# Gate rows by way of DRAM, six inner values read back during "up", the last two chunks of "down" multiplied bank by bank

## Chip, cores and metric

The kernel runs on one core of a Trainium2 chip. The metric is the device time of one execution in microseconds (us); the time of a kernel is the median of its runs.

## What is computed

One transformer block of 512 tokens (S) and width 2048 (D), in fp32: adaptive layer norm from a condition vector c, a mixer of short convolution and sparse attention, and a gated feed-forward part of width 5632 (FF). The change touches where the two gate vectors g_a and g_f come in, and the last product.

```python
sh_a, sc_a, g_a, sh_f, sc_f, g_f = jnp.split(jax.nn.silu(c) @ ada_w[l] + ada_b[l], 6, axis=-1)
...
x = x + g_a[:, None, :] * (jnp.concatenate([y_conv, y_attn], axis=-1) @ w_out[l])
h = modulate(rms_norm(x, norm_ffn[l]), sh_f, sc_f)
x = x + g_f[:, None, :] * ((jax.nn.silu(h @ ffn_w1[l]) * (h @ ffn_w3[l])) @ ffn_w2[l])
```

## The kernel before

Every large fp32 product is done in three TensorE products of a split operand: ScalarE casts a high part (`whi` of a weight, `phi` of an activation), VectorE subtracts it for the low part (`wlo`, `plo`), and TensorE adds low·high, high·low and high·high into one PSUM bank.

The stages follow each other: the mixer with its projections, the output product with w_out ("o", about 705 to 893 us), the second norm, the gated pair w1, w3 ("up", 905 to 1782), and w2 ("down", to the end).

**"o" and "down"** share the function `products`. It splits both operands into 2 x 2 blocks and forms seven block products (passes p = 1, 5, 6, 3, 7, 2, 4) for each group of chunks of 128 rows: two groups of four chunks in "o", four groups of 6, 6, 5 and 5 in "down". The unit of the order is a step (group b, pass p, chunk k): 12 matmuls, three for each of four banks (`multiply`, L965). Two passes run in turn on two sets of four banks, called main and aux. For a step two places ahead the function emits the split of the activation (`a_split`: for p = 5 a difference `u` of the tiles g1 and g0, L935, and always `phi` L946 and `plo` L947) and of the weight (`w_split`: `whi` L919, `wlo` L921), and a GpSimd DMA (L927, queue POOL) that adds the next weight block to the weight tile in place. `start_loads` issues the weight and g loads on SyncE's queue (SP), each as soon as its ring has room. The rings hold three `whi` and `wlo` and six of the activation's parts. A scheduler then orders the instructions of each engine; an engine takes them strictly in that order.

**In "up"**, the units u = 0 to 43 run passes of the same kind on the normed activations `hC` (L1187 with whi, L1189 with wlo). Their results, 44 tiles `d` of 128 x 512, go to DRAM (`gd`), and "down" reads them back as g0 and g1 (L1419), seven of each at a time. These rings lie in memory that the operands of "up" use, the block `hC1` (pool stack `hst`) among them; `hC1` is last used by the last step with p = 1.

**The gates.** Each gate vector exists first as columns (`gac`, `gfc`: 128 partitions x 16). The product with a token-major result needs it as rows, the same 2048 values in all 128 partitions (`ga`, `gf`). `gate_rows` makes them: for each of 16 blocks VectorE forms a diagonal matrix `dg` (L291), TensorE multiplies a matrix of ones with it (L292; the profile counts two TensorE rows for each), and ScalarE copies each finished bank (L293). It is called in a hook at (b, p, k) = (0, 7, 2) of "o" with bank set main, and at (0, 1, 1) of "down" with aux. `ga` is first read when the first results of "o" are scaled, `gf` in the last group of "down". At the end, the last pass (p = 4) of the last group multiplies each bank by `gf` (L1435), adds it to y (L1436) and stores it (L1441).

Of the kernel before, what the change touches and what calls it, by code (L numbers as in the profile page):

```python
# [10 lines left out]
F32 = mybir.dt.float32  # L11
# [3 lines left out]
ALU = mybir.AluOpType  # L15
# [3 lines left out]
P = 128  # L19
D = 2048  # L20
S = 512
# [50 lines left out]
def block_kernel(ctx: ExitStack, tc: tile.TileContext, a: dict, out: bass.AP):  # L72
# [153 lines left out]
    def sums_stream():  # L226

        jobs = [(lambda acc, n=n: gate_cols(acc, n, 0, gac), 2 * D + n * 512) for n in range(4)]
        for j in range(8):
            m = 1 - j % 2  # L230
            jobs.append((lambda acc, m=m, j=j: ada_cols(main if j == 7 else aux, acc, 1, m, j // 2 * 4, 4), (3 + m) * D + j // 2 * 512))
        at_job, late = 0, None
        for e, (turn_, c0) in enumerate(jobs):
            acc = accp.tile([P, 512], F32, tag=f"acc{e % 2}", name=f"acc{e % 2}")
            for k in range(KC):
                w = spare[0]()
                with tc.issue_after(latest["load"]):
                    nc.sync.dma_start(w, ada_v[:, k, c0:c0 + 512])
                with tc.issue_after(latest["lo"]):
                    if k:  # L240
                        nc.vector.scalar_tensor_tensor(acc, w, cT[:, k:k + 1], acc, op0=ALU.mult, op1=ALU.add)
                    else:
                        nc.vector.tensor_scalar(acc, w, cT[:, k:k + 1], None, op0=ALU.mult)
                if late and k == 2:
                    late[0](late[1])
                yield
            late = turn_, acc
        late[0](late[1])

    def gate_steps(temp, lag):  # L250

        for n in range(4):
            acc = accp.tile([P, 512], F32, tag="acc0", name="acc0")
            for k in range(KC):
                w = temp() if k else acc
                with tc.issue_after(latest["load"]):
                    nc.sync.dma_start(w, ada_v[:, k, 5 * D + n * 512:5 * D + (n + 1) * 512])
                for _ in range(lag // 2):
                    yield
                with tc.issue_after(latest["hi"]):  # L260
                    nc.scalar.activation(w, w, AF.Copy, scale=cT[:, k:k + 1])
                if k:
                    nc.gpsimd.dma_start(acc, w, accum_op=ALU.add)
                for _ in range(lag - lag // 2):
                    yield
            gate_cols(acc, n, 1, gfc)

    def gate_cols(acc, n, which, to):

# [12 lines left out]
            nc.vector.tensor_reduce(d, v, axis=AX, op=ALU.add, negate=True)  # L282
            nc.vector.tensor_sub(d, d, b)

    def gate_rows(row, col, tile_of, temp):

        for n in range(4):
            ps = tile_of()
            for c in range(4):
                dg = temp.tile([P, P], F32, tag="dg", name="dg", bufs=2)  # L290
                nc.vector.tensor_scalar(dg, ident, col[:, 4 * n + c:4 * n + c + 1], None, op0=ALU.mult)  # L291
                nc.tensor.matmul(ps[:, c * P:(c + 1) * P], ones, dg, start=True, stop=True)  # L292
            nc.scalar.copy(row[:, n * 512:(n + 1) * 512], ps)  # L293

    pp = pool("ps", 4, space=PSUM)
    main = lambda: pp.tile([P, S], F32, tag="main", name="main")
# [573 lines left out]
    qk.close()  # L870
    act_.close()

    dram = ctx.enter_context(tc.tile_pool(name="spill", bufs=1, space=bass.MemoryType.DRAM))
    xd = [dram.tile([P, NT, 512], F32, name=f"xd{n}") for n in range(4)]
    gd = [dram.tile([P, S], F32, name=f"gd{f}") for f in range(FF // P)]
    HS, HK = S // 2, KC // 2
# [1 line left out]
    BLOCK = {1: (0, 0), 2: (0, 0), 5: (1, 1), 7: (1, 1), 6: (0, 1), 3: (0, 1), 4: (1, 0)}  # L878
    FIRST, LAST = (1, 5, 6, 4), (2, 7, 3, 4)

    def products(w, groups, order, flip, new_w, room, T, t_loads, G0, G1, g_loads, parts_, sums, read, hook):

        steps = [(b, p, k) for b, (top, _) in enumerate(groups) for p in order[b] for k in range(len(top))]
        where = {s: i for i, s in enumerate(steps)}
# [10 lines left out]
        for b, (top, _) in enumerate(groups):  # L895
            for p in (3, 2):
                for k in range(len(top)):
                    loads["w"].append(((b, 7 if p == 3 else 2, k), lambda n, b=b, p=p, k=k: load_w(n, b, p, k)))
        begun = {q: 0 for q in loads}

        def start_loads(done, most, which=("g0", "t", "g1", "w")):

# [47 lines left out]
        def multiply(i):  # L950

            b, p, k = steps[i]
            n_k = len(groups[b][0])
            chain = "x" if p in (1, 6, 7, 4) else "y"
            begins = p in (1, 5, 2) and k == 0
            ends_ = p in (4, 3, 2) and k == n_k - 1
            if begins:
                make = main if (chain == "x") == (b % 2 == flip) else aux
                banks[chain] = [make() for _ in range(4)]
            wt, at_k = split_w.pop(i), split_a.pop(i)  # L960
            for e, ps in enumerate(banks[chain]):
                tok = slice((e // 2) * P, (e // 2 + 1) * P)
                cs = slice((e % 2) * 512, (e % 2 + 1) * 512)
                for m, (l, r) in enumerate(((0, 1), (1, 0), (0, 0))):
                    nc.tensor.matmul(ps, at_k[l][:, tok], wt[r][:, cs], start=begins and m == 0, stop=ends_ and m == 2,  # L965
                                     skip_group_check=True)
            note("mm")
            if k == n_k - 1:
                reads.extend((b, p, e, ps) for e, ps in enumerate(banks[chain]))
# [133 lines left out]
    def o_hook(b, p, k):  # L1103

        if (b, p, k) == (0, 1, 0):
            with tc.issue_after(latest["o_hi"]), tc.issue_after(latest["o_lo"]):
                next(rest[0])
        if (b, p, k) == (0, 1, 1):
            with tc.issue_after(latest["o_lo"]):
                next(stream, None)  # L1110
        if (b, p, k) == (0, 7, 0):
            next(rest[0], None)
        if (b, p, k) == (0, 7, 2):
            gate_rows(ga, gac, main, tp)
        if b and p == 2:
            scaled()
        if b and p == 7:
            if k == 0:
                for i in (2, 3):
                    for n in range(2):  # L1120
                        cs = slice(n * 512, (n + 1) * 512)
                        nc.vector.tensor_mul(y2[:, i, cs], y2[:, i, cs], ga[:, cs])
                        nc.gpsimd.dma_start(y2[:, i, cs], x[i * P:(i + 1) * P, cs], accum_op=ALU.add)
            scaled()
            for _ in range((1, 2, 2, 3)[k]):
                x2_store(*turns.pop(0))
        if b and p == 4:
            if k == 0:
                row_norms(0)
            scaled()  # L1130
            x2_store(*turns.pop(0))
            if k > 1:
                modulated(0, 0, 4 * k - 8, aux)
                split_half(0, 0, 4 * k - 8)
# [235 lines left out]
    t2p = pool("t2", 1, stack=ust)  # L1370
    gtp = pool("gate", 1, stack=ust)
    gate = gate_steps(lambda: gtp.tile([P, 512], F32, tag="graw", name="graw"), 4)
    for n, s in enumerate(order):
        for m in range(n + 5, n + 1, -1):
            if m < len(order) and lead[id(order[m])] == m - n:
                prepare(m, "sum")
        if n + 5 < len(order):
            begin(order[n + 5]["u"])
        if n > 2:
            prepare(n + 2, "split")  # L1380
        if n < 4 * PLAIN:
            h_sums(n)
        s["mm"](s, (1,) if n < 3 else (0, 1)) if n < 4 * PLAIN else s["mm"](s)
        if 0 < n < 3:
            prepare(n + 2, "split")
        s["post"](s)
        if n >= 8 * PLAIN:
            next(gate, None)
    for _ in gate:
        pass  # L1390
    ust.close()
    hst.close()


    GROUPS, at0 = [], 0
    for n in (6, 6, 5, 5):
        GROUPS.append((range(at0, at0 + n), range(at0 + n, at0 + 2 * n)))
        at0 += 2 * n
    GM = 6
    pap = pool("parts", 6)  # L1400
    rgp = pool("graw", GM + 1)
    xsp = pool("xsum", GM + 1)
    wxp = pool("wraw", 5)
    yp = pool("y2", 1)
    y2 = yp.tile([P, NT, D], F32, name="y2")
    gf = yp.tile([P, D], F32, name="gf")
    tp = pool("tmp2", 4)
    T, G0, G1 = {}, {}, {}

    def load_t(b, k):  # L1410
        pair = big()
        for e in range(min(2, len(GROUPS[b][0]) - k)):
            T[b, k + e] = pair[:, e * 1024:(e + 1) * 1024]
            f = GROUPS[b][0][k + e]
            nc.sync.dma_start(T[b, k + e], w2[f * P:(f + 1) * P, 0:1024])

    def load_g(to, j, b, k):
        to[b, k] = rgp.tile([P, S], F32, tag=f"g{j}", name=f"g{j}")
        nc.sync.dma_start(to[b, k], gd[GROUPS[b][j][k]])  # L1419

    every_k = [(b, k) for b, (top, _) in enumerate(GROUPS) for k in range(len(top))]
    t_loads = [((b, 4, min(k + 1, len(top) - 1)), lambda n, b=b, k=k: load_t(b, k))
# [23 lines left out]

    def d_hook(b, p, k):

        if (b, p, k) == (0, 1, 1):
            gate_rows(gf, gfc, aux, tp)  # L1450
        if (b, p, k) == (len(GROUPS) - 1, 7, 0):
            for i in (2, 3):
                for n in range(2):
                    cs = slice(n * 512, (n + 1) * 512)
                    nc.vector.tensor_mul(y2[:, i, cs], y2[:, i, cs], gf[:, cs])
                    nc.gpsimd.dma_start(y2[:, i, cs], xd[n][:, i, :], accum_op=ALU.add)

    products(w2, GROUPS, ((1, 5, 6, 3, 7, 2, 4),) * 4, 0,
             lambda n: (ring[0] if n % 9 in (0, 2, 4, 6) else wxp).tile([P, 1024], F32, tag="raw", name="raw"),
             {"t": 4, "w": 9, "g0": GM + 1, "g1": GM + 1}, T, t_loads, G0, G1, g_loads, pap, xsp, d_read, d_hook)  # L1460


# [22 lines left out]
```

## Time and profile before

| what | us |
|---|---|
| median of three runs | 2224.24 |
| their spread | 2221.83 to 2224.64 |
| the profiled execution's own time | 2223.04 |
| its span | 2221.3 |

The span runs from the first to the last instruction of the profiled execution; about 1.7 us of its own time lie outside it. In the profile, PE is TensorE's matmul side and PEld its weight loads, DVE is VectorE, ACT ScalarE, POOL GpSimd, SP SyncE (SPq: the time it takes to issue). A row of a timeline has its start, its length, the engine, the line, the operation with output and inputs, the partitions and elements, a count, and in brackets how long the engine stood idle before and what ended that wait. A row of the chain of waits has a start, a length and what the end of the program hung on in that stretch. The figure in PEclk is the clock that TensorE was granted, as a share of full speed.

### The profile page before, as it was taken

Reading aid. Unit: us, or ns where it says so; the run is one execution under the profiler, and the core shown is the slowest. Engines: PE = TensorE matmul, PEld = TensorE weight load, DVE = VectorE, ACT = ScalarE, POOL = GpSimd, SP = SyncE. Lnnn points to the kernel's source line nnn. Section 1 sums busy time; section 2 is a strip of 40 time slices with the busy share of each in tenths; the row PEclk is TensorE's granted clock in tenths of the full one; section 3 lists DMA queues with packets and bytes.
Section 4 is the critical chain, followed back from the end, with each engine's and each line's share of the span. In section 5 each row is a group of like instructions: output and inputs, shape, how many; then the busy total and the mean of one; then the engine's idle time right before and its main releaser. Section 6 shows DMA issues by size and latency. Waiting matters only on the chain.

```text
span 2221.3 us, 30757 instructions
## 1 busy us (share of the span) xinstructions
PE 2150.8 (97%) x10999; PEld 1805.2 (81%) x10999; DVE 1797.8 (81%) x2795; ACT 1110.0 (50%) x1863; POOL 273.5 (12%) x321
## 2 busy tenths in 40 slices
PE   5899999999999999899999999999999989999998
PEld 5677778878778787788888888888888878888887
DVE  5888868878878787698888888888888876878787
ACT  6545334554543554745555555555554455554543
POOL 2330000000000223101110110110110021211132
PEclk9999999999999999999999999999999999999999
DMA  8885775645558968366665665666665399898897
GB/s 296 293 264 173 236 245 177 187 140 150 153 169 250 227 147 182 114 183 171 175 172 161 166 163 155 170 163 165 172 165 149 128 265 232 212 229 204 223 183 181
DMA packets 387550, 421.57 MB, mean 190 GB/s; under 512 B 19808, under 2 KB 293572, under 8 KB 386884
## 3 DMA queue, kind: packets, MB, share of 16 engines
q1 hardware_dynamic: 352068, 316.82, 45.8%
q0 software_dynamic: 35328, 102.78, 23.5%
q8 instruction: 86, 1.41, 0.3%
q14 instruction: 68, 0.56, 0.1%
HBM read 383.87 MB, written 19.92 MB: 182 GB/s over the span
## 4 chain that ended last, share of the span: by engine, by line
PE 82%; DVE 6%; DMA 6%; issue 3%; ACT 1%; POOL 1%; SPq 0%; DVEq 0%; POOLq 0%; ACTq 0%
PE main L1187 15%; PE aux L1187 11%; PE main L965 10%; PE aux L965 10%; PE main L1189 8%; PE aux L1189 6%; PE main L108 5%; PE main L110 5%; PE main L109 5%; PE aux L783 2%; DMA t<-in_w_out 1%; PE aux L755 1%; DMA y<-in_x 1%; DVE acc L326 1%; DMA raw<-in_w_in 1%
## 5 line engine op out<-in xcount | busy, mean ns | idle before, releaser
L1187 PE MATMUL main<-hC,whi 128*128 128x512 f32 x1408 | 355.1, 394 | 0.0
L1187 PEld LDWEIGHTS main<-hC,whi 128*128 128x128 f32 x1408 | 253.6, 189 | 46.0 <-DVE hC L1054 0.5
L1187 PE MATMUL aux<-hC,whi 128*128 128x512 f32 x1072 | 268.6, 392 | 0.0
L1187 PEld LDWEIGHTS aux<-hC,whi 128*128 128x128 f32 x1072 | 192.6, 189 | 34.0
L1180 DVE TENSOR_TENSOR wlo<-xy,whi 128x1024 fp32r<-128x1024 f32 x135 | 164.5, 1219 | 64.3 <-ACT whi L1174 64.2
L1174 ACT CAST whi<-xy 128x1024 fp32r<-128x1024 f32 x135 | 141.5, 1048 | 146.8 <-PE main L1187 76.8
L108 PE MATMUL main<-alo,whi 128*128 128x512 f32 x448 | 185.4, 414 | 22.0 <-DVE alo L396 22.0
L1189 PEld LDWEIGHTS main<-hC,wlo 128*128 128x128 f32 x1408 | 192.2, 190 | 14.3
L1189 PE MATMUL main<-hC,wlo 128*128 128x256 f32 x1408 | 196.2, 282 | 0.0
L109 PE MATMUL main<-ahi,wlo 128*128 128x512 f32 x448 | 179.2, 400 | 0.0
L110 PE MATMUL main<-ahi,whi 128*128 128x512 f32 x448 | 179.1, 400 | 0.0
L965 PE MATMUL main<-wlo,phi 128*128 128x512 f32 x420 | 167.1, 399 | 12.3 <-ACT phi L946 4.5
L965 PE MATMUL main<-whi,phi 128*128 128x512 f32 x420 | 166.0, 395 | 0.0
L965 PE MATMUL main<-whi,plo 128*128 128x512 f32 x420 | 166.0, 395 | 0.0
L965 PE MATMUL aux<-wlo,phi 128*128 128x512 f32 x420 | 164.3, 391 | 0.0
L965 PE MATMUL aux<-whi,plo 128*128 128x512 f32 x420 | 163.6, 390 | 0.0
L965 PE MATMUL aux<-whi,phi 128*128 128x512 f32 x420 | 163.5, 389 | 0.0
L1189 PEld LDWEIGHTS aux<-hC,wlo 128*128 128x128 f32 x1072 | 146.2, 190 | 10.5
L919 ACT CAST whi<-raw 128x1024 fp32r<-128x1024 f32 x90 | 94.9, 1055 | 114.7 <-PE aux L965 60.0
L1174 ACT CAST whi<-t 128x1024 fp32r<-128x1024 f32 x84 | 88.2, 1049 | 123.1 <-PE aux L1187 63.2
L919 ACT CAST whi<-xy 128x1024 fp32r<-128x1024 f32 x88 | 92.9, 1055 | 113.4 <-PE main L965 55.4
L1189 PE MATMUL aux<-hC,wlo 128*128 128x256 f32 x1072 | 149.5, 282 | 0.0
(341 smaller groups left out, 4488.7 us busy)
## 6 DMA issues: line engine op xcount, KB each, us to landing
xy<-in_ffn_w SPq DMA_DIRECT2D x130, 512.0 KB, 4.8
raw<-in_ffn_w SPq DMA_DIRECT2D x112, 512.0 KB, 5.1
araw<-in_ada_w SPq DMA_DIRECT2D x208, 256.0 KB, 4.0
xy<-in_ffn_w POOLq DMA_DIRECT2D x66, 512.0 KB, 6.3
raw<-in_w_in SPq DMA_DIRECT2D x128, 192.0 KB, 2.9
raw<-in_w_in SPq DMA_DIRECT2D x40, 512.0 KB, 6.0
xy<-in_ada_w SPq DMA_DIRECT2D x80, 256.0 KB, 4.3
graw<-in_ada_w SPq DMA_DIRECT2D x60, 256.0 KB, 2.8
```

What stands on the lines that cost most here:

```text
L108: nc.tensor.matmul(ps, lhs[0], rhs[1], start=first, stop=False)
L109: nc.tensor.matmul(ps, lhs[1], rhs[0], start=False, stop=False)
L110: nc.tensor.matmul(ps, lhs[0], rhs[0], start=False, stop=last)
L326: nc.vector.scalar_tensor_tensor(acc, w, s, acc, op0=ALU.mult, op1=ALU.add)
L755: nc.tensor.matmul(one[b], queries(g, i, h), kT[b][g][:, :L], start=True, stop=True)
L783: nc.tensor.matmul(po[:, b * HD:(b + 1) * HD], s["pT"][b][:, kb * P:(kb + 1) * P], vv[b][:, kb, g * HD:(g + 1) * HD], start=kb == 0, stop= ...
L919: nc.scalar.copy(hi, wt)
L965: nc.tensor.matmul(ps, at_k[l][:, tok], wt[r][:, cs], start=begins and m == 0, stop=ends_ and m == 2, skip_group_check=True)
L1174: nc.scalar.copy(hi, t)
L1180: nc.vector.tensor_sub(lo, t, hi.bitcast(F32))
L1187: nc.tensor.matmul(ps, wt[0][:, ks[k]], hC[p][:, k, :], start=first and k == 0, stop=False, skip_group_check=True)
L1189: nc.tensor.matmul(ps[:, HS:], wt[1][:, ks[k]], hC[p][:, k, 0:HS], start=False, stop=last and k == HK - 1, skip_group_check=True)
```

## The change

There are three parts.

1. `gate_rows` is gone. `gate_out` turns the columns by one TensorE transpose (128 x 16 to 16 x 128), VectorE copies the result into a free accumulator, and a GpSimd DMA stores its 8 KB in DRAM (`grow`). `gate_in` is one SyncE DMA that reads `grow` into all 128 partitions (1 MB written). For `ga`, `gate_out` stands in the stream that sums the gates during attention, `gate_in` at step (0, 6, 0) of "o". For `gf`, `gate_out` follows the last gate columns in "up", and `gate_in` stands at step (1, 1, 0) of "down".
2. `hst` is closed right after the last step with p = 1 in "up" instead of after "up". The g0 ring gets a pool of its own in that memory, and its first six loads are issued there; `products` is told by `begun` that six are under way. The g1 ring stays where both were.
3. In `multiply`, the last step but one returns at once, and the last step does both chunks bank by bank: six matmuls for the first bank, then six for the next.

```diff
+    def gate_out(which, col, psum_tile, acc):
+        ps = psum_tile()
+        nc.tensor.transpose(ps[:KC, :P], col, ident)
+        gt = acc[:KC, 0:P]
+        nc.vector.tensor_copy(gt, ps[:KC, :P])
+        nc.gpsimd.dma_start(grow[which].rearrange("o (k p) -> (o k) p", p=P), gt)
+
+    def gate_in(which, row):
+        nc.sync.dma_start(row, grow[which].to_broadcast([P, D]))
...
                 if late and k == 2:
                     late[0](late[1])
+                    if e == 4:
+                        gate_out(0, gac, aux, late[1])
...
             gate_cols(acc, n, 1, gfc)
+        gate_out(1, gfc, main, acc)
...
-        begun = {q: 0 for q in loads}
+        begun = {q: (begun or {}).get(q, 0) for q in loads}
...
-            wt, at_k = split_w.pop(i), split_a.pop(i)
+            if i == len(steps) - 2:
+                return
+            at_once = (i - 1, i) if i == len(steps) - 1 else (i,)
             for e, ps in enumerate(banks[chain]):
                 tok = slice((e // 2) * P, (e // 2 + 1) * P)
                 cs = slice((e % 2) * 512, (e % 2 + 1) * 512)
-                for m, (l, r) in enumerate(((0, 1), (1, 0), (0, 0))):
-                    nc.tensor.matmul(ps, at_k[l][:, tok], wt[r][:, cs], start=begins and m == 0, stop=ends_ and m == 2,
-                                     skip_group_check=True)
+                for j in at_once:
+                    wt, at_k = split_w[j], split_a[j]
+                    for m, (l, r) in enumerate(((0, 1), (1, 0), (0, 0))):
+                        nc.tensor.matmul(ps, at_k[l][:, tok], wt[r][:, cs], start=begins and m == 0,
+                                         stop=ends_ and j == i and m == 2, skip_group_check=True)
...
-        if (b, p, k) == (0, 7, 2):
-            gate_rows(ga, gac, main, tp)
+        if (b, p, k) == (0, 6, 0):
+            gate_in(0, ga)
...
+        if n == last_1:
+            hst.close()
+            rings_g[0] = pool("gtop", GM + 1, side="right")
+            for early in range(1, GM + 1):
+                load_g(G0, 0, 0, early - 1)
     for _ in gate:
         pass
     ust.close()
-    hst.close()
...
-        if (b, p, k) == (0, 1, 1):
-            gate_rows(gf, gfc, aux, tp)
+        if (b, p, k) == (1, 1, 0):
+            gate_in(1, gf)
```

Where the instructions stand. First, VectorE at the beginning of "down", before (numbers tell tiles apart; g0 and g1 are the tiles from DRAM, phi and plo the parts of the first pass's operand, u the differences for pass 5):

```order
L947 TENSOR_TENSOR plo_16223<-g0_16194,phi_16222 128x256
L935 TENSOR_TENSOR u_16412<-g1_16199,g0_16194 128x256
L947 TENSOR_TENSOR plo_16232<-g0_16201,phi_16231 128x256
L935 TENSOR_TENSOR u_16437<-g1_16206,g0_16201 128x256
L935 TENSOR_TENSOR u_16460<-g1_16213,g0_16208 128x256
L947 TENSOR_TENSOR plo_16241<-g0_16208,phi_16240 128x256
L921 TENSOR_TENSOR wlo_16282<-xy_16203,whi_16281 128x1024
L947 TENSOR_TENSOR plo_16278<-g0_16215,phi_16277 128x256
```

And the same place after the change (L953 is the plo of L947, L941 the u of L935, L927 the wlo of L921; L1300 finishes the last tile of "up"):

```order
L953 TENSOR_TENSOR plo_16187<-g0_15969,phi_16186 128x256
L953 TENSOR_TENSOR plo_16196<-g0_15971,phi_16195 128x256
L1300 SCALAR_TENSOR_TENSOR d2_16002<-d2_16002,d1_15962 128x512
L953 TENSOR_TENSOR plo_16205<-g0_15973,phi_16204 128x256
L953 TENSOR_TENSOR plo_16238<-g0_15975,phi_16237 128x256
L953 TENSOR_TENSOR plo_16265<-g0_15977,phi_16264 128x256
L953 TENSOR_TENSOR plo_16290<-g0_15979,phi_16289 128x256
L941 TENSOR_TENSOR u_16314<-g1_16169,g0_15969 128x256
L941 TENSOR_TENSOR u_16339<-g1_16174,g0_15971 128x256
L941 TENSOR_TENSOR u_16362<-g1_16179,g0_15973 128x256
L927 TENSOR_TENSOR wlo_16242<-xy_16171,whi_16241 128x1024
```

All six plo of the first pass now stand together ahead of the first u, and three u stand in a row ahead of the low weight part of that pass's fourth chunk (wlo_16242).

Second, SyncE's DMA issues at the end of "up", before (g0, g1 from the tiles gd in DRAM, xy the first weight blocks of "down"):

```order
L1415 DMA xy_16210<-in_ffn_w2 128x1024 x2
L1415 DMA xy_16217<-in_ffn_w2 128x1024 x2
L1419 DMA g0_16194<-gd0_6467 128x512
L1419 DMA g1_16199<-gd6_6473 128x512
L1419 DMA g0_16201<-gd1_6468 128x512
L1419 DMA g1_16206<-gd7_6474 128x512
```

And after (L1395 is the g load of L1419, L1437 the weight load of L1415, L898 a weight load of the ring `raw`):

```order
L898 DMA raw_16298<-in_ffn_w2 128x1024
L1395 DMA g0_15969<-gd0_6473 128x512
L1395 DMA g0_15971<-gd1_6474 128x512
L1395 DMA g0_15973<-gd2_6475 128x512
L1395 DMA g0_15975<-gd3_6476 128x512
L1395 DMA g0_15977<-gd4_6477 128x512
L1395 DMA g0_15979<-gd5_6478 128x512
L1395 DMA g0_16164<-gd12_6485 128x512
L1437 DMA xy_16176<-in_ffn_w2 128x1024 x2
L1437 DMA xy_16181<-in_ffn_w2 128x1024 x2
L1395 DMA g1_16169<-gd6_6479 128x512
L1395 DMA g1_16174<-gd7_6480 128x512
```

The g0 loads have moved ahead of the xy loads; the first of them waits for the last matmuls with p = 1 in "up", and the g1 loads follow one another where g0 and g1 alternated.

Third, SyncE in "o", after the change (before, the same raw loads stood there without the L300 row; the brackets name the semaphores that an issue waits for):

```order
L898 DMA raw_6658<-in_w_out 128x1024 [waits DMAHW5_49,DVE_49]
L898 DMA raw_6660<-in_w_out 128x1024 [waits DMAHW6_49]
L898 DMA raw_6685<-in_w_out 128x1024 [waits DMAHW7_49,DVE_49,Activation_49]
L300 DMA ga_6536<-grow0_103 128x2048 [waits DMAHW0_49,DMASW0_49]
L898 DMA raw_6949<-in_w_out 128x1024 [waits DMAHW1_49,DMASW5_49,DVE_49]
```

The load of `ga` stands behind the first group's raw loads and ahead of those of the second.

Elsewhere the order moves little. The load of `gf` stands in "down" behind five raw loads and ahead of the second group's g0 loads. Near 1700 us TensorE's transpose of the gate goes between two passes of the last unit but one. At the end of "o", the first group of transposes of the normed rows (L1065) stands ten matmuls earlier. At the very end, VectorE's four multiplications (L1435) and four additions (L1436) alternate bank by bank instead of two by two.

More of the change, by code (lines that the diff above doesn't have):

```diff
@@ L283, in gate_cols @@
             nc.vector.tensor_sub(d, d, b)
[L285 to L293, printed above, removed]
+    dram = ctx.enter_context(tc.tile_pool(name="spill", bufs=1, space=bass.MemoryType.DRAM))
+    grow = [dram.tile([1, D], F32, name=f"grow{n}") for n in range(2)]
+    def gate_out(which, col, psum_tile, acc):
[6 more added lines that the diff above has]
+        nc.sync.dma_start(row, grow[which].to_broadcast([P, D]))
     pp = pool("ps", 4, space=PSUM)
@@ L871, in block_kernel @@
     act_.close()
-    dram = ctx.enter_context(tc.tile_pool(name="spill", bufs=1, space=bass.MemoryType.DRAM))
     xd = [dram.tile([P, NT, 512], F32, name=f"xd{n}") for n in range(4)]
@@ L879, in block_kernel, with products @@
     FIRST, LAST = (1, 5, 6, 4), (2, 7, 3, 4)
-    def products(w, groups, order, flip, new_w, room, T, t_loads, G0, G1, g_loads, parts_, sums, read, hook):
+    def products(w, groups, order, flip, new_w, room, T, t_loads, G0, G1, g_loads, parts_, sums, read, hook, begun=None):
         steps = [(b, p, k) for b, (top, _) in enumerate(groups) for p in order[b] for k in range(len(top))]
@@ L963, in multiply @@
                 cs = slice((e % 2) * 512, (e % 2 + 1) * 512)
-                for m, (l, r) in enumerate(((0, 1), (1, 0), (0, 0))):
-                    nc.tensor.matmul(ps, at_k[l][:, tok], wt[r][:, cs], start=begins and m == 0, stop=ends_ and m == 2,
-                                     skip_group_check=True)
+                for j in at_once:
[3 more added lines that the diff above has]
+                                         stop=ends_ and j == i and m == 2, skip_group_check=True)
+            for j in at_once:
+                del split_w[j], split_a[j]
             note("mm")
@@ L1372, in block_kernel, with load_g @@
     gate = gate_steps(lambda: gtp.tile([P, 512], F32, tag="graw", name="graw"), 4)
+    GROUPS, at0 = [], 0
+    for n in (6, 6, 5, 5):
+        GROUPS.append((range(at0, at0 + n), range(at0 + n, at0 + 2 * n)))
+        at0 += 2 * n
+    GM = 6
+    T, G0, G1 = {}, {}, {}
+    rings_g = {}
+    def load_g(to, j, b, k):
+        to[b, k] = rings_g[j].tile([P, S], F32, tag=f"g{j}", name=f"g{j}")
+        nc.sync.dma_start(to[b, k], gd[GROUPS[b][j][k]])
+    last_1 = max(n for n, s in enumerate(order) if s["p"] == 1)
+    early = 0
     for n, s in enumerate(order):
@@ L1391, in block_kernel @@
     ust.close()
-    hst.close()
[L1395 to L1399, printed above, removed]
     pap = pool("parts", 6)
-    rgp = pool("graw", GM + 1)
+    rings_g[1] = pool("graw", GM + 1)
     xsp = pool("xsum", GM + 1)
@@ L1407, in block_kernel @@
     tp = pool("tmp2", 4)
-    T, G0, G1 = {}, {}, {}
     def load_t(b, k):
@@ L1415, in load_t @@
             nc.sync.dma_start(T[b, k + e], w2[f * P:(f + 1) * P, 0:1024])
-    def load_g(to, j, b, k):
-        to[b, k] = rgp.tile([P, S], F32, tag=f"g{j}", name=f"g{j}")
-        nc.sync.dma_start(to[b, k], gd[GROUPS[b][j][k]])
     every_k = [(b, k) for b, (top, _) in enumerate(GROUPS) for k in range(len(top))]
@@ L1459, in block_kernel @@
              lambda n: (ring[0] if n % 9 in (0, 2, 4, 6) else wxp).tile([P, 1024], F32, tag="raw", name="raw"),
-             {"t": 4, "w": 9, "g0": GM + 1, "g1": GM + 1}, T, t_loads, G0, G1, g_loads, pap, xsp, d_read, d_hook)
+             {"t": 4, "w": 9, "g0": GM + 1, "g1": GM + 1}, T, t_loads, G0, G1, g_loads, pap, xsp, d_read, d_hook, {"g0": early})
 INS = ["x", "c", "positions", "ada_w", "ada_b", "norm_mix", "norm_ffn", "w_in", "conv_w", "cmp_pe_k", "cmp_k_w1",
```

## The prediction

> **What bounds the kernel now.** I read the page first, then the chain of waits, then timeline and windows at the four places that the diff touches.
>
> ```profile
> span 2221.3 us, 30757 instructions
> PE 2150.8 (97%) x10999; PEld 1805.2 (81%) x10999; DVE 1797.8 (81%) x2795; ACT 1110.0 (50%) x1863; POOL 273.5 (12%) x321
> PE 82%; DVE 6%; DMA 6%; issue 3%; ACT 1%; POOL 1%; SPq 0%; DVEq 0%; POOLq 0%; ACTq 0%
> ```
>
> TensorE is busy 97% of the span and makes 82% of the chain. So a removed matmul is worth its time, and otherwise only the places where TensorE stands still can be won. The beginning of "down" is one. The chain there:
>
> ```profile
> 1759.55 1.86 PE main L1187 x8
> ...
> 1780.02 13.21 DMA g<-gd
> ...
> 1793.26 0.41 ACT phi L946
> ...
> 1793.71 4.83 PE main L965 x12
> ...
> 1812.71 16.32 PE aux L965 x72
> ```
>
> Pass 1 (into main) ends at 1812.71, where pass 5 begins. An undisturbed pass of six steps is 72 matmuls, 16.32 us (2.72 a step, 0.227 a matmul). "Up" ends at 1781.74, so pass 1 takes 31 us: its operand waits for the g tiles that return from DRAM. The timelines of TensorE, ScalarE, VectorE and SyncE there:
>
> ```profile
> 1781.74 0.60 PE L292 MATMUL aux<-dg,const 128*128 128x128 f32 x4
> ...
> 1787.58 1.59 PE L965 MATMUL main<-wlo,phi 128*128 128x512 f32 x3 [3.00 <-ACT phi L946]
> ...
> 1793.71 0.51 PE L965 MATMUL main<-wlo,phi 128*128 128x512 f32 x1 [1.52 <-ACT phi L946]
> ...
> 1797.92 0.39 PE L965 MATMUL main<-whi,plo 128*128 128x512 f32 x1
> ```
> ```profile
> 1782.25 0.35 ACT L1197 COPY d<-main 128x256 f32<-128x256 f32 x1
> ...
> 1787.12 0.40 ACT L946 CAST phi<-g 128x256 fp32r<-128x256 f32 x1 [3.05 <-DMA g<-gd]
> ```
> ```profile
> 1790.67 0.43 DVE L935 TENSOR_TENSOR u<-g,g 128x256 f32<-128x256 f32 x1 [2.69 <-DMA g<-gd]
> ...
> 1796.27 1.23 DVE L921 TENSOR_TENSOR wlo<-xy,whi 128x1024 fp32r<-128x1024 f32 x1 [0.29 <-ACT whi L919]
> ```
> ```profile
> 1779.14 15.05 SPq L1419 DMA_DIRECT2D g<-gd  x12
> ```
>
> The waits read: the first three g loads of this queue, begun from 1779.14, landed at about 1787.0 (first phi), 1790.6 (first u) and 1793.2 (second phi). Clock and transfers show in windows (columns: busy PE, PEld, DVE, ACT, POOL; clock; DMA share; GB/s):
>
> ```profile
> 1756.00:1762.00 6.00, 6.00 (x38) 5.31 (x37) 6.00 (x9) 2.81 (x4) 0.00 (x0) 1.00 0.03 12
> ...
> 1780.00:1784.00 4.00, 2.47 (x18) 2.12 (x17) 2.97 (x6) 1.97 (x4) 1.29 (x2) 1.00 0.99 203
> 1788.00:1792.00 4.00, 4.00 (x12) 2.93 (x11) 0.43 (x1) 0.00 (x0) 0.00 (x0) 0.61 1.02 234
> ```
>
> After 3.00 us of standing still the granted clock is 0.61, and after the second wait ten matmuls take from 1793.71 to 1797.92, 4.2 us instead of 2.27.
>
> **The change part by part.**
>
> *The row of the first gate (ga).* Timeline of TensorE, the group in the stretch 772.7 to 784, two windows ("o" and the start), a DMA issue, the queue, and one step of pass 6:
>
> ```profile
> 772.82 0.61 PE L292 MATMUL main<-dg,const 128*128 128x128 f32 x4
> 775.62 0.71 PE L292 MATMUL main<-dg,const 128*128 128x128 f32 x4 [1.27 <-DVE dg L291]
> 781.28 0.48 PE L965 MATMUL main<-wlo,phi 128*128 128x512 f32 x1
> 793.18 0.39 PE L965 MATMUL aux<-wlo,phi 128*128 128x512 f32 x1
> ```
> ```profile
> L292 PE MATMUL main<-dg,const 128*128 128x128 f32 x32 | 5.7, 295 | 1.7 <-DVE dg L291 1.7
> ```
> ```profile
> 742.00:746.00 4.00, 4.00 (x18) 3.31 (x19) 2.87 (x6) 4.00 (x8) 1.72 (x2) 1.00 1.05 205
> 5.00:8.00 3.00, 0.00 (x0) 0.00 (x0) 0.00 (x0) 1.90 (x3) 0.00 (x0) 1.00 1.03 431
> ```
> ```profile
> xy<-in_x SPq DMA_DIRECT2D x4, 1024.0 KB
> ```
> ```profile
> q1 hardware_dynamic: 352068, 316.82, 45.8%
> ```
> ```profile
> 743.08 1.23 DVE L921 TENSOR_TENSOR wlo<-t,whi 128x1024 fp32r<-128x1024 f32 x1 [0.47 <-ACT whi L919]
> ```
> ```profile
> 744.72 0.39 PE L965 MATMUL aux<-wlo,phi 128*128 128x512 f32 x1
> ```
>
> From 772.82 to 781.28, 8.46 us, only 12 of the stage's own matmuls run (2.72): 5.74 us are the gate's. The next pass, four steps, takes 781.28 to 793.18 = 11.90 instead of 10.88, another 1.02. So 6.76 us go. What comes is one load of 1 MB at pass 6, behind the six w_out loads that stand ahead of it in the queue, in a stretch where the DMA share is 1.05 (the row at 742): there it displaces other transfers. At the 431 GB/s of the row at 5.00, where loads of the same shape run alone, 1 MB takes 2.43 us. In pass 6 a weight split ends at 744.31 and its matmul begins at 744.72: 0.4 us of slack. So I take 2.5 lost, between 0 and 3.4 (1.05 of the queue's 316.82 MB, times 45.8% of 2221.3). Net **-4.3**, bounds -6.8 to -3.4.
>
> [...]
>
> *Early g0 loads and the second gate (gf).* The first six g0 loads now wait for the last p = 1 step of "up" (1759.55) instead of the end of "up". The DMA share between 1756 and 1762 is 0.03, so 1.5 MB finds room, and they are there well before 1780. ScalarE makes the first phi right after its copy at 1782.25: TensorE starts pass 1 at about 1783.0 instead of 1787.58, after 1.3 us of standing, and the row at 775.62 (1.27) was followed by no slow spacing. Three steps run to 1791.2. Then VectorE is late: in its new order three u differences, each waiting for a g1 tile, stand ahead of the wlo of the fourth step. The g1 tiles now take the first three places of the queue, 1787.0, 1790.6 and 1793.2 by the rows above; the third u ends at 1793.6, wlo (1.23) at 1794.9. TensorE stands 3.7 us and starts at half clock: as after 1793.71, ten slow matmuls, 2.0 us lost. The other three steps (8.16) end at 1794.9 + 8.16 + 2.0 = 1805.06 instead of 1812.71: **-7.65**. Without this wait pass 5 would start at 1783.0 + 16.4 = 1799.4, -13.3; with g1 another 2.6 us later, -5. The gf products, of which the row at 1781.74 shows the first, stand inside pass 1 and are in these differences. The gf load comes at pass 1 of the second group; I take 0, since nine raw tiles let the weight loads run ahead there; without this cover, up to 3.4.
>
> [...]
>
> *What the gate costs now.* Timeline of TensorE in "up":
>
> ```profile
> 1700.27 0.60 PE L273 MATMUL main<-const,acc 128*128 128x128 f32 x4
> 1700.63 1.64 PE L1187 MATMUL main<-hC,whi 128*128 128x512 f32 x6
> ```
>
> Four transposes take 0.36, so two cost 0.2. The VectorE copies and the POOL stores stand beside matmuls; no row shows whether TensorE waits for the last gate column, so 0 to 0.5 more: **+0.3**.
>
> *The end.* Timelines of VectorE and TensorE:
>
> ```profile
> 2214.88 0.39 PE L965 MATMUL aux<-whi,phi 128*128 128x512 f32 x1
> ```
> ```profile
> 2208.24 1.23 DVE L921 TENSOR_TENSOR wlo<-xy,whi 128x1024 fp32r<-128x1024 f32 x1
> ...
> 2213.27 1.37 DVE L1435 TENSOR_TENSOR t<-aux,gf 128x512 f32<-128x512 f32 x2 [3.81 <-PE aux L965]
> ...
> 2216.96 1.28 DVE L1436 TENSOR_TENSOR y<-y,t 128x512 f32<-128x512 f32 x2
> ```
>
> Four products and four additions follow almost all matmuls and end at 2218.24. With six matmuls a bank, 1.36 us, a bank's pair (1.3) fits beneath the next bank's; only the last pair is left: 2215.3 + 1.3 = 2216.6. **-1.6**. The last weight split is now needed 4.8 us before the last matmul ends (2210.5) instead of 2.7; it ended at 2209.47, which still does: cost 0, and up to 1 if it slips by two.
>
> *The end of "o".* The order moves one group of transposes (L1065) ahead of ten matmuls.
>
> ```profile
> 898.06 2.08 PE L1065 MATMUL aux<-dn,y 128*128 128x128 f32 x8 [3.53 <-ACT xy L1069]
> ```
>
> TensorE waits there anyway, in both orders; I take 0, bounds -3 to +3.5 (the wait of this row once lost or doubled).
>
> **Sum**: -6.76 + 2.5 - 7.65 + 0.3 - 1.6 = -13.2, against this profiled execution's own 2223.04 (its span and 1.7 us around it): 2209.8. That execution lies 1.2 below the median of 2224.24. I forecast **2210**.
>
> **Rivals.**
> *The wait for g1 does not bite* (it lands earlier, since the g0 traffic is gone from its queue): -13.3 instead of -7.65, **2204**. For it: half of the twelve loads are away. Against it: the first three places took until 1793.2 although little was ahead of them.
> *The ga load and the new order at the end of "o" eat what the removed products gave*: 2209.8 + 4.3 = **2214**. For it: the DMA share of 1.05 and the 0.4 us of slack. [...]
> *The change does not do what it says*: if the six loads are held by another buffer's wait until the end of "up", the 7.65 are gone: **2217.4**. Against it: in the new order they stand directly on the wait for the last p = 1 matmuls.
> *Slower: the broadcast.* Each gate row is read 128 times from one 8 KB place in DRAM. If this runs slowly and holds all queues, both loads cost their whole time. Without load costs the sum is -15.7, so it decides from 7.9 us a load (133 GB/s). At 95 GB/s, 11 us each, the time is **2229**. The nearest rows, of all DMA issues:
>
> ```profile
> gains<-in_k_norm SPq DMA_DIRECT2D x3, 64.0 KB, 3.1
> per<-in_cmp_pe_k SPq DMA_DIRECT2D x1, 16.0 KB, 2.9
> ```
>
> A broadcast of 64 KB lands 0.2 later than a plain 16 KB, which speaks against it; sixteen times 3.1 would be 50 us, which is why I keep it.
>
> **How the numbers follow.** Forecast (2206 to 2212) 0.45; g1 early 0.20; "o" eats its gain 0.20; no early loads 0.06; slow broadcast 0.06; others 0.03. About 0.2%, 4.4 us, is what a measurement of this kernel can tell from no change. Faster by more (below 2219.8): the first three cases but for 0.02, and half of the fourth, 0.86; within it, 0.08; slower, 0.06. The range must reach both 2204 and 2217: **2202 to 2218**.
>
> **What would show it.** Pass 5 of the first group begins at about 1805 minus what "o" has gained; before it, TensorE stands twice, 1.3 and then 3 to 4 us, the second wait ended by wlo and VectorE's u before it by the g1 load. A single wait would make it the first rival. Between the start of pass 7 and of pass 4 in "o" 6.8 us are missing, and some of it comes back as waits in passes 6 and 3 for a whi or wlo whose accumulate is late. The last VectorE row ends 1.3 us after the last matmul. The forecast fails most likely by the load of ga (no row shows a 1 MB broadcast from DRAM), or by the g1 tiles' place among other transfers.

## The result and the profile after

The changed kernel took 2210.53 us in the median of four runs (2207.83 to 2211.75), beside 2223.72 for the kernel before: ratio 0.9946, interval 0.9933 to 0.9958. Its profiled execution took 2209.42 us, span 2207.7. Two executions far outside the others, one of 10554.33 us in experiment e2 and one of 4379.13 us in e10, are left out of the medians in this document. From its page, the span, the engines and the shares of the chain:

```profile
span 2207.7 us, 30603 instructions
PE 2136.6 (97%) x10937; PEld 1793.0 (81%) x10937; DVE 1793.2 (81%) x2765; ACT 1105.9 (50%) x1855; POOL 274.9 (12%) x323
PE 84%; DMA 6%; DVE 5%; issue 2%; ACT 2%; POOL 1%; SPq 0%; POOLq 0%; ACTq 0%; DVEq 0%
```

62 TensorE rows are gone (64 of the gates' products less two transposes). The rest must be read stage by stage. First "o", TensorE's timeline, before:

```profile
714.78 0.48 PE L965 MATMUL aux<-wlo,phi 128*128 128x512 f32 x1
...
752.88 0.39 PE L965 MATMUL main<-wlo,phi 128*128 128x512 f32 x1
```

And after:

```profile
712.16 0.48 PE L975 MATMUL aux<-wlo,phi 128*128 128x512 f32 x1
...
741.92 0.80 PE L975 MATMUL aux<-wlo,phi 128*128 128x512 f32 x1 [2.23 <-DVE wlo L927]
754.55 0.39 PE L975 MATMUL main<-wlo,phi 128*128 128x512 f32 x1
...
777.21 0.39 PE L975 MATMUL main<-wlo,phi 128*128 128x512 f32 x1
788.09 0.39 PE L975 MATMUL aux<-wlo,phi 128*128 128x512 f32 x1
```

From the start of pass 3 (754.55) to that of pass 4 (788.09) it is 33.54 us, before 793.18 - 752.88 = 40.30: 6.76 less, the figure of the gate products to the hundredth (the two other kernels that keep them, e2 and e3 below, have 40.25 and 39.55, so the hundredth is luck). But from the start of "o" (712.16) to pass 3 it is 42.39 instead of 38.10, with a new wait of 2.23 us at the start of pass 6, ended by a wlo, and a half-clock stretch behind it (granted clock 0.51 from 742.00 to 745.40 us, before 1.00).

Then the beginning of "down", TensorE, the start of pass 5 before:

```profile
1812.55 0.39 PE L965 MATMUL aux<-wlo,phi 128*128 128x512 f32 x1
```

And after:

```profile
1774.05 1.11 PE L1201 MATMUL main<-hC,wlo 128*128 128x256 f32 x8
1776.23 1.28 PE L975 MATMUL main<-wlo,phi 128*128 128x512 f32 x4 [1.07 <-ACT phi L952]
...
1790.59 0.80 PE L975 MATMUL main<-wlo,phi 128*128 128x512 f32 x1 [3.01 <-DVE wlo L927]
...
1796.30 0.57 PE L975 MATMUL main<-whi,plo 128*128 128x512 f32 x1
...
1798.99 0.39 PE L975 MATMUL aux<-wlo,phi 128*128 128x512 f32 x1
```

And VectorE:

```profile
1779.41 1.09 DVE L941 TENSOR_TENSOR u<-g,g 128x256 f32<-128x256 f32 x3
...
1785.33 0.42 DVE L941 TENSOR_TENSOR u<-g,g 128x256 f32<-128x256 f32 x1 [2.83 <-DMA g<-gd]
1788.64 0.43 DVE L941 TENSOR_TENSOR u<-g,g 128x256 f32<-128x256 f32 x1 [2.89 <-DMA g<-gd]
...
1789.31 1.22 DVE L927 TENSOR_TENSOR wlo<-xy,whi 128x1024 fp32r<-128x1024 f32 x1
```

"Up" ends where the 1.07 us of waiting begins, at 1775.16; pass 5 begins at 1798.99, 23.83 us later, before 30.81 (1781.74 to 1812.55). TensorE stands twice: 1.07 us for phi, then 3.01 for a wlo that VectorE reaches only behind two u, each waiting for a g1 tile.

The end, VectorE's and TensorE's last rows and windows (busy PE, PEld, DVE, ACT, POOL; clock; DMA share; GB/s):

```profile
2202.48 0.69 DVE L1454 TENSOR_TENSOR y<-y,t 128x512 f32<-128x512 f32 x1
```
```profile
2201.33 0.39 PE L975 MATMUL aux<-whi,phi 128*128 128x512 f32 x1
```
```profile
2201.00:2202.50 1.50, 0.71 (x4) 0.25 (x2) 1.43 (x4) 0.00 (x0) 0.00 (x0) 1.00 0.08 26
2202.50:2206.00 3.50, 0.00 (x0) 0.00 (x0) 0.67 (x1) 0.00 (x0) 0.00 (x0) 1.00 0.97 375
2206.00:2207.70 1.70, 0.00 (x0) 0.00 (x0) 0.00 (x0) 0.00 (x0) 0.00 (x0) 0.58 0.00 0
```

VectorE ends 1.45 us after the last matmul (2203.17 - 2201.72), before 2.97 (2218.24 - 2215.27). Yet the span ends 5.9 us after that matmul, before 6.0: from 2202.5 to 2206 the DMA engines move 375 GB/s x 3.5 us = 1.3 MB, five stores of 256 KB in one block, after having stood nearly still. The trace shows why: the first of the five stores a tile of y onto which a GpSimd DMA (L1458) adds another from DRAM, and this addition lands at 2201.71; SyncE issues that store at 2201.73 and the other four, whose tiles do not need it, behind it.

### The profile page after: what moved, and what is told of

Read it like the earlier page. It is cut to its first block, busy times and chain, and to the rows that moved or that the text cites. A ratio compares the mean times of both kernels' runs of the same rounds, so it can differ in the third digit from the quotient of the medians.

```text
span 2207.7 us, 30603 instructions
## 1 busy us (share of the span) xinstructions
PE 2136.6 (97%) x10937; PEld 1793.0 (81%) x10937; DVE 1793.2 (81%) x2765; ACT 1105.9 (50%) x1855; POOL 274.9 (12%) x323
## 3 DMA queue, kind: packets, MB, share of 16 engines
q0 software_dynamic: 35392, 102.79, 23.5%
## 4 chain that ended last, share of the span: by engine, by line
PE 84%; DMA 6%; DVE 5%; issue 2%; ACT 2%; POOL 1%; SPq 0%; POOLq 0%; ACTq 0%; DVEq 0%
PE main L1199 15%; PE aux L1199 11%; PE aux L975 11%; PE main L975 10%; PE main L1201 8%; PE aux L1201 6%; PE main L108 5%; PE main L110 5%; PE main L109 5%; DMA t<-in_w_out 2%; PE aux L790 2%; PE aux L762 1%; DMA y<-in_x 1%; DMA raw<-in_w_in 1%; DVE acc L333 1%
```

## Experiments

In the table, "o to p3" is the time from the start of "o" to its pass 3, "p3 to p4" from there to pass 4, "up to p5" from the end of "up" to pass 5 of "down", and "tail" from the end of the last matmul to the end of the span, each in the profiled execution (in the kernel before and e3, where TensorE goes on without a wait, "up" ends where the next product starts). The ratio is to the kernel before as it was measured beside the row, with its interval: its median was 2223.72 us beside the changed kernel, 2221.66 beside e1 to e4, 2221.95 beside e5 to e8 and 2222.31 beside e9 to e12. So rows are compared by their ratios first.

| kernel | median us | ratio | o to p3 | p3 to p4 | up to p5 | tail |
|---|---|---|---|---|---|---|
| before | 2223.72 | | 38.10 | 40.30 | 30.81 | 6.0 |
| changed | 2210.53 | 0.9946 (0.9933 to 0.9958) | 42.39 | 33.54 | 23.83 | 5.9 |
| changed again (e12) | 2209.14 | 0.9943 (0.9931 to 0.9955) | 41.39 | 33.54 | 23.21 | 6.0 |
| part 1 alone (e1) | 2210.41 | 0.9946 (0.9934 to 0.9958) | 40.87 | 33.54 | 24.55 | 6.5 |
| part 2 alone (e2) | 2216.43 | 0.9979 (0.9968 to 0.9990) | 38.76 | 40.25 | 26.42 | 6.0 |
| part 3 alone (e3) | 2219.93 | 0.9987 (0.9978 to 0.9997) | 39.02 | 39.55 | 31.40 | 4.7 |
| ga load twice (e4) | 2211.80 | 0.9955 (0.9940 to 0.9970) | 42.74 | 33.60 | 23.36 | 6.2 |
| ga hook later (e5) | 2211.35 | 0.9952 (0.9940 to 0.9964) | 41.00 | 33.54 | 23.06 | 5.1 |
| u behind wlo (e6) | 2206.09 | 0.9930 (0.9918 to 0.9942) | 39.52 | 33.54 | 17.70 | 5.3 |
| last stores on ScalarE (e7) | 2209.22 | 0.9944 (0.9932 to 0.9957) | 41.88 | 33.54 | 23.06 | 5.2 |
| e5, e6, e7 together (e8) | 2204.05 | 0.9930 (0.9916 to 0.9943) | 38.57 | 33.54 | 17.63 | 5.3 |
| ga behind raw loads (e9) | 2209.94 | 0.9946 (0.9934 to 0.9957) | 39.39 | 33.54 | 24.37 | 6.0 |
| part 1 with u behind wlo (e10) | 2212.35 | 0.9955 (0.9942 to 0.9968) | 42.60 | 33.54 | 23.25 | 6.4 |
| changed, u behind wlo, ga behind raws (e11) | 2202.42 | 0.9915 (0.9902 to 0.9928) | 37.63 | 33.54 | 17.64 | 5.7 |

### The parts alone

**e1**, only the first part of the diff.

> The first part alone (both gates as rows by way of DRAM; g loads and the last two chunks as before). Theory A (the ga load of 1 MB takes its place among the accumulates of 'o'): the row products of ga leave, -6.8 us between the start of passes 7 and 4; the load shows as a VectorE wlo wait of about 2 us at the start of pass 6 and a half-clock window behind it, +3 to +4.5. At the start of 'down' the gf products leave pass 1, about -3. Together -5 to -7: 2217 to 2219. Theory B (that wait came by chance and the load is hidden): no wait over 1 us at pass 6, together about -10: 2214.

2210.41, ratio 0.9946: as much as the whole change gains, by its first part. The wait in "o" is there, though as two waits and without half clock behind them (granted clock 1.00 from 742.00 to 745.40, and "o to p3" is no longer than before plus the two waits, 41.83):

```profile
741.17 0.50 PE L971 MATMUL aux<-wlo,phi 128*128 128x512 f32 x1 [2.04 <-DVE wlo L927]
...
745.88 0.50 PE L971 MATMUL aux<-wlo,phi 128*128 128x512 f32 x1 [1.69 <-DVE wlo L927]
```

At "down":

```profile
1779.28 0.73 PE L971 MATMUL main<-wlo,phi 128*128 128x512 f32 x2 [2.77 <-ACT phi L952]
...
1788.30 0.59 PE L971 MATMUL main<-wlo,phi 128*128 128x512 f32 x1 [3.24 <-ACT phi L952]
...
1801.06 0.39 PE L971 MATMUL aux<-wlo,phi 128*128 128x512 f32 x1
```

TensorE still waits for g0, 2.77 and 3.24 us, but without the gf products pass 5 begins 24.55 us after "up" (1776.51) instead of 30.81: they had cost twice what was expected here. So the stretches come to -6.3 at "down", -6.8 + 2.8 in "o". Theory A held on the load's wait, but not on the half clock, and 2.8 us are just below its 3 to 4.5; its gain of 5 to 7 was 4 to 6 too small, half of that by the gf products.

**e2**, only the early loads.

> The second part alone (six early g0 loads; gates by products, tail as before). Theory A (the early loads start pass 1 of 'down' about 6 us sooner, and then one wait of VectorE for g1 takes some of it back): from the end of 'up' to the start of pass 5 about 25 to 28 us instead of 31, since the gf products partly fall into the wait; time -3 to -6, 2218 to 2221. Theory B (most of the gain at 'down' was the removed gf products, not the loads): 30 us or more, time within 1.5 of before.

```profile
1785.53 1.28 PE L965 MATMUL main<-wlo,phi 128*128 128x512 f32 x4 [1.07 <-ACT phi L946]
...
1793.54 0.71 PE L292 MATMUL aux<-dg,const 128*128 128x128 f32 x4 [1.88 <-DVE dg L291]
...
1810.88 0.39 PE L965 MATMUL aux<-wlo,phi 128*128 128x512 f32 x1
```

The first wait is 1.07 us as in the changed kernel, and then the gate products stand in the way. 26.42 us, -4.4 against before: theory A. Part 1 gives -6.3 there, part 2 -4.4, both together -7.0: they win largely the same time.

**e3**, only the bank-by-bank end.

> The third part alone (last two chunks bank by bank). Theory A (the last four stores stand on SyncE's queue behind one that waits for a POOL accumulate, so that VectorE's earlier end wins nothing): the span still ends 5.8 to 6.4 us after the last matmul; time within 0.5 of before. Theory B (the step of the prediction): the span ends about 4.4 us after it; time -1.6.

```profile
2215.96 0.39 PE L969 MATMUL aux<-whi,phi 128*128 128x512 f32 x1
```

The span of 2221.1 ends 4.7 us after this matmul, not 5.8 to 6.4: near theory B here, and the ratio is just below 1. Yet the order of theory A is there: SyncE issues the last five stores from 2215.51, right after the last addition from DRAM has landed at 2215.49, here 0.86 us before the last matmul ends. In the eight profiles with this part and the stores on SyncE's queue the tail lies between 4.7 and 6.2, mean 5.6; in the four without it between 6.0 and 6.5, mean 6.2. It wins about 0.6 us. In those eight the tail follows that landing: 4.7 where it came 0.86 us before the end of the last matmul (e3), 5.9 where it came with it (changed), 6.2 where it came 0.37 behind it (e4), and the others in order between.

### The ga load

**e4**: `gate_in(0, ga)` issued twice in the hook at (0, 6, 0).

> The changed kernel with the ga load issued twice, one behind the other, at the same place. Theory A (the load delays the accumulates by its own transfer time, 2.4 us or more): the waits before the ends of passes 5, 6 and 3 in 'o' grow by 2.4 to 4 us together against the changed kernel; time 2213 to 2215. Theory B (hidden load): the start of pass 3 lies where it lies in the changed kernel, 42.4 us after the start of 'o'; time 2210 to 2211.

```profile
744.17 0.66 PE L975 MATMUL aux<-wlo,phi 128*128 128x512 f32 x1 [2.32 <-DVE wlo L927]
756.77 0.39 PE L975 MATMUL main<-wlo,phi 128*128 128x512 f32 x1
```

42.74 us, hardly more than with one load: a miss for theory A's size. SyncE issued the second load only 25 us after the first, and its packets came from 746.7 to 752.6, behind the start of pass 6 (744.17), in which TensorE then waits no more.

**e5**: the hook moved from (0, 6, 0) to (0, 4, 0).

> The changed kernel with the ga load moved to pass 4 of the first group of 'o', behind the stretch in which accumulates fill the DMA engines. Theory A (the load costs about 3 us there, through the accumulates): from the start of 'o' to the start of pass 3 it is 38 to 39.2 us as without the load, instead of 40.9 to 42.4, and no pass behind it is longer than 10.9; -3 against the changed kernel, 2207 to 2208. Theory B (those differences are chance): 41 us or more again; 2210 to 2211.

41.00 us, no gain; but SyncE issued the load at the same place as before (720.32, where the changed kernel has 717.53), so the later hook had not moved it. This run tells nothing on the load, and serves as one more profile with it.

**e9** holds the place by an order:

```diff
-        if (b, p, k) == (0, 6, 0):
-            gate_in(0, ga)
+        if (b, p, k) == (0, 4, 0):
+            with tc.issue_after(latest["w_load"]):
+                gate_in(0, ga)
```

> The changed kernel with the ga load ordered behind the last w_out load of the second group (in the run called e5 its place on SyncE's queue had stayed the same, so that one said nothing on it). Theory A (the load costs about 3 us where it stands, through the accumulates): 38 to 39.2 us from the start of 'o' to the start of pass 3 instead of 40.9 to 42.4, the passes behind it not over 10.9; -2 to -4 against the changed kernel. Theory B: 41 us or more again, no gain.

SyncE's and TensorE's timelines, and ScalarE's at the first `whi` of pass 6:

```profile
779.90 0.43 SPq L300 DMA_DIRECT2D ga<-grow  x1
```
```profile
742.42 0.39 PE L976 MATMUL aux<-wlo,phi 128*128 128x512 f32 x1
753.30 0.39 PE L976 MATMUL main<-wlo,phi 128*128 128x512 f32 x1
```
```profile
739.65 1.05 ACT L926 CAST whi<-t 128x1024 fp32r<-128x1024 f32 x1 [1.09 <-DMA t<-in_w_out]
```

The same cast in the unchanged repetition of the changed kernel (e12), with the load in its first place:

```profile
739.58 1.04 ACT L925 CAST whi<-t 128x1024 fp32r<-128x1024 f32 x1 [4.49 <-DMA t<-in_w_out]
```

Issued at 779.90, the load leaves pass 6 at its 10.88 us and "o to p3" at 39.39. The five profiles with one load in that stretch and the old order of u (changed, e1, e5, e7, e12) have 40.9 to 42.4, mean 41.5; the four without it (before, e2, e3, e9) 38.1 to 39.4, mean 38.8. The load costs 2.7 us, theory A, and the casts show the way: ahead of this one ScalarE stands 3.6 to 4.5 us with the load and 1.1 to 1.8 without it, as the accumulate of t comes late. With u behind wlo (below) the cost is less even: 42.60, 39.52 and 38.57 with the load (e10, e6, e8), 37.63 without (e11). In the time of the whole kernel e9 shows no gain (ratio 0.9946 as the changed one): 2 us are within the interval, and its own pass 1 of "down" was 0.9 above the mean.

### The wait for g1

**e6**:

```diff
             if p == 5:
                 U[b, k] = sums.tile([P, HS], F32, tag="u", name="u")
-                nc.vector.tensor_sub(U[b, k], g1[:, half[1]], g0[:, half[1]])
+                with tc.issue_after(latest["o_lo"]):
+                    nc.vector.tensor_sub(U[b, k], g1[:, half[1]], g0[:, half[1]])
```

> The changed kernel with each u difference of pass 5 ordered behind the wlo emitted before it, so that VectorE waits for no g1 tile ahead of a wlo of pass 1. Theory A (this order is what TensorE's second wait at the start of 'down' hangs on): from the end of 'up' to the start of pass 5 17.4 to 18.5 us instead of 23.4 to 23.8, and no slow clock there; -5.5 against the changed kernel, 2204 to 2206. Theory B (the g1 loads are late for pass 5 as well, and the wait only moves): 21 us or more up to the start of pass 5 or new waits over 1 us inside it; 2208 to 2211.

```profile
1773.27 1.28 PE L976 MATMUL main<-wlo,phi 128*128 128x512 f32 x4 [1.07 <-ACT phi L953]
...
1789.90 0.39 PE L976 MATMUL aux<-wlo,phi 128*128 128x512 f32 x1
```

1789.90 - 1773.27 is 16.63, nearly an undisturbed pass (16.32); with the 1.07 ahead 17.70. Theory A: the second wait hung on this order alone. But part of the gain comes back later. Passes 6 and 7 of the first group now take 17.14 and 18.97 us instead of 16.32, and from the start of pass 5 to the last matmul it is 406.19 us instead of 402.72. There ScalarE waits for accumulated weight blocks, and TensorE behind it:

```profile
1853.42 1.05 ACT L925 CAST whi<-raw 128x1024 fp32r<-128x1024 f32 x1 [2.52 <-DMA raw<-in_ffn_w]
```
```profile
1855.79 0.50 PE L976 MATMUL main<-wlo,phi 128*128 128x512 f32 x1 [0.85 <-DVE wlo L927]
```

In the changed kernel, which gets to pass 7 some 8 us later, the casts wait for TensorE alone:

```profile
1856.31 1.05 ACT L925 CAST whi<-raw 128x1024 fp32r<-128x1024 f32 x1 [1.36 <-PE main L975]
```

So 3.5 of the 5.8 us at the start are lost again to the GpSimd DMAs, and "down" as a whole wins 2.3. e8 and e11 show the same (406.11 and 405.98); the ten kernels with the old order have 402.7. The edit stands in `products` and so moves u in "o" as well; what it does there ("o to p3" 39.52 here, 42.60 in e10) stays open. 2206.09 is at the slow edge of what was expected.

**e10**: e6's edit on part 1 alone, so without the early loads.

> The first part alone, with u ordered behind wlo, so without the early g0 loads. Theory A (early loads and order of u need each other: with u ahead of wlo the g1 wait takes the place of the g0 wait, without it the early loads are worth their 6 us): from the end of 'up' to the start of pass 5 23 to 25 us, as in the first part alone, waits ended by ScalarE's phi and g0 loads; 2209 to 2211. Theory B (the order of u alone matters, the early loads little): 18 to 20 us; 2204 to 2206.

```profile
1779.72 1.22 PE L972 MATMUL main<-wlo,phi 128*128 128x512 f32 x2 [3.10 <-ACT phi L953]
...
1799.87 0.39 PE L972 MATMUL aux<-wlo,phi 128*128 128x512 f32 x1
```

23.25 us: theory A. With u ahead of wlo the early loads are worth 24.55 - 23.5 = 1.1 us beside part 1 (23.5 is the mean of six changed kernels), with u behind it 23.25 - 17.65 = 5.6. Two waits stood one behind the other, and removing one alone mostly uncovers the other. Here too later waits take some back (404.33 us from pass 5 to the last matmul): "down" from the end of "up" to the last matmul is 427.3 in e1, 427.6 in e10, 426.2 in the changed kernels and 423.7 with both (e6, e8, e11). The time fits: with 2212.35 e10 is no faster than e1, and just slower than either theory said.

### The last stores, and all together

**e7**: the last four stores by `nc.scalar.dma_start`.

> The changed kernel with the last four stores issued from ScalarE's queue. Theory A (they stand behind a store that waits for a POOL accumulate): the span ends 4.3 to 4.9 us after the last matmul instead of 5.9 to 6.2; -1.3 against the changed kernel. Theory B (the end is the time of the DMA itself): 5.8 or more, time within 0.5 of the changed kernel.

A tail of 5.2 lies between the two theories and inside the spread of 4.7 to 6.2: not decided. The last store is now issued 0.03 us after VectorE's last row instead of 0.46, but the span still ends 3.72 us after that issue, before the change 3.01.

**e8**: the edits of e5, e6 and e7.

> The changed kernel with the three edits together: ga loaded at pass 4, u behind wlo, last stores on ScalarE's queue. If the three lie on the path one after the other, their sum, -3 - 5.6 - 1.3 = -10: 2200 to 2202. If they share a wait, less than two thirds of it: 2204 or more.

2204.05, less than the sum: as in e5, the ga load had not moved. Its 17.63 repeats e6, and its ratio too (0.9930).

**e11**: e6 and e9 together.

> The changed kernel with u behind wlo and ga behind the last w_out load. From the start of 'o' to pass 3 37 to 39 us, from the end of 'up' to pass 5 17.4 to 18.5. If the two add, -6 - 2 against the changed kernel: 2202 to 2204; if u behind wlo had already removed what the ga load costs, as the 39.5 us of 'o' in the run with u alone suggest, -6: 2205.

Both stretches are as expected (37.63 and 17.64). 2202.42, ratio 0.9915, is the fastest of all, beyond the interval of the changed kernel (0.9931 to 0.9955 for e12, measured beside it). That the two add is likely but not shown: "o to p3" is 1.9 us below e6 and 0.9 below e8, against 2.1 between e9 and the five kernels above, and the intervals of e6 and e11 overlap.

**e12**:

> The changed kernel once more, for the stages beside the others of this call: 40.9 to 42.4 us from the start of 'o' to pass 3, 23.4 to 23.9 from the end of 'up' to pass 5, the span 5.1 to 6.2 after the last matmul; 2209 to 2212.

41.39 and 6.0 are as expected, 23.21 a little below; the wait for wlo in pass 1 is 3.64 us here.

## Why the prediction was right

The forecast was 2210, the time 2210.53. Taken by its steps:

- **ga products**, -6.76: 33.54 instead of 40.30. Right.
- **ga load**, +2.5: 2.7 by the four profiles without it, e9 among them. Right in size, and the way that was given: a wlo wait at pass 6, behind a late accumulate.
- **Start of "down"**, -7.65: -7.0 in the profile, -7.3 by the mean of six changed kernels. The mechanism was right (an early first wait, then a wlo behind u behind g1), two details were not: the first three g1 tiles were there by 1780, so the wait came one step later, at the fifth chunk; and the slow stretch was longer, 13 matmuls from 1790.59 to 1796.30, 5.7 us instead of 2.95 (granted clock 0.50 from 1790 to 1794), a loss of 2.8 and not 2.0. The two nearly cancel.
- **What it was put down to** was wrong: the prediction held the gf products to be inside this step, and its rival without early loads lost the whole -7.65 (2217.4). e1 shows -6.3 without any early load; on top of part 1 they are worth 1.1.
- **End of "o"**, 0, and **the gate's new cost**, +0.3: from pass 4 of "o" to the end of "up" it is 987.0 to 989.2 us, mean 987.9, in the ten profiles with part 3 (`multiply` is shared, so the last two steps of "o" run bank by bank too, which is what moves the transposes), and 988.4 to 989.2, mean 988.7, in the four without; with part 1 987.0 to 989.2, without it 988.6 to 989.2. No loss shows for either.
- **The end**, -1.6: this term was mis-sized. VectorE did end 1.5 us sooner after TensorE, but the step took the span to end as long after VectorE as before (3.0 us). The last stores stand on SyncE's queue behind one that waits for the addition from DRAM, and go out in one block: the span ends 4.5 us after VectorE, and wins only about 0.6 in the mean.
- The rival "slower by the broadcast" fell: the loads of 8 KB rows cost 2.7 us in "o" and nothing visible in "down", whose passes after the first are 16.32 us as before; an effect inside the first pass is not excluded.

The profiled executions differ by 13.6 us. By stages: -6.76 + 4.3 - 1.5 - 7.0 - 0.1 = -11.1, and -2.6 up to the start of "o", which were there at the 1201st matmul already (297.05 and 294.40), ahead of any changed instruction. So the close hit of the number holds some chance.

## What to carry over

When two engines' waits stand one behind the other ahead of the same pass, price a removal by what becomes late next, and try the pair: beside part 1 the early loads alone gave 1.1 us up to pass 5, the order of u alone 1.3 (24.55 to 23.25), both 6.9 (to 17.64). Then measure to the end of the stage: there both together gave 3.6 (427.3 to 423.7), because the engine that got ahead met the next limit, the accumulates (in e6 a cast stands 2.52 us for one). A transfer that replaces engine work can have its own price: here the load of `ga` cost 2.7 us, that of `gf` nothing visible. And moving the call is not moving the transfer (e5, issued at 720.32 instead of 717.53): see in the trace where the issue stands. A stage that gains at one engine can give it back at the stores that close the program: here VectorE ended 1.5 us sooner after TensorE, and the span won about 0.6.

## What was not expected of the hardware

**The same instructions, 6 us apart.** The 1201st matmul of the trace, at about 297 us and ahead of any changed instruction (TensorE's order first differs at about 401 us), begins between 292.8 and 298.7 us in the fourteen profiles. Half-clock stretches fall differently. Windows of the kernel before and of e8:

```profile
100.00:190.00 90.00, 81.47 (x342) 65.35 (x341) 77.62 (x113) 35.57 (x51) 22.72 (x18) 0.94 0.80 256
```
```profile
100.00:190.00 90.00, 81.09 (x360) 65.08 (x359) 81.41 (x120) 39.99 (x57) 22.88 (x19) 1.00 0.79 257
```

The mean clock is 0.94 in one and 1.00 in the other, with 18 fewer rows in the same 90 us. The kernels without part 1 lie among the later ones (297.1 to 298.7); with three of them, whether something else than chance is in it stays open.

**Short waits can be enough.** The trace of before has half clock behind waits of 3.00 and 1.52 us (0.58 from 1787.58 to 1791.60, 0.59 from 1793.71 to 1797.92), and none behind 1.27 us (1.00 from 774 to 779). After the change the 2.23 us in "o" and the 3.01 us in "down" were followed by half clock (0.51 and 0.50 in the windows below), the 1.07 us were not (1.00 from 1775.16 to 1780.00):

```profile
742.00:745.40 3.40, 3.40 (x8) 2.72 (x9) 2.49 (x5) 3.03 (x6) 1.30 (x2) 0.51 1.07 211
```
```profile
1790.00:1794.00 4.00, 3.41 (x8) 2.74 (x9) 2.58 (x7) 0.00 (x0) 0.87 (x1) 0.50 1.03 385
```

In e12 a longer wait at the same place in "o" was not: behind it the matmuls begin 0.23 us apart (742.28 to 744.61 for ten), in the changed kernel 0.43 (742.52 to 745.08 for six), and pass 6 took 11.59 us there instead of 12.63:

```profile
741.94 0.50 PE L975 MATMUL aux<-wlo,phi 128*128 128x512 f32 x1 [2.81 <-DVE wlo L927]
```

The clock's records tell the two apart. In all fourteen traces the clock changes only on a grid of 3.41 us (in before and after, 32 of 32 clock records last a whole number of these; the last record of each trace, which ends with it, is left aside). Of the grid's stretches at full clock, all 85 in which TensorE was busy less than 0.43 of the time were followed by half clock, and none of the 8651 in which it was busy more than 0.56; between, 8 of 61 were (before and after alone: 15 of 15, none of 1236, 2 of 8). The 2.23 us fell into one stretch (busy 0.35), the 2.81 us into two (0.71 and 0.47). So whether a wait of 2 to 3 us cost its own length or up to about twice that depended here on how it lay to the grid.
